# Instance norm over 512 channels: loads of two units at once on SP's queue, and the last unit's sum divided between VectorE and ScalarE

## The chip, the cores and the metric

One core of a Trainium2 chip. The metric is the device time of one execution in microseconds (us); lower is better. The median of 3 runs of the kernel before is 626.86 us (626.76 to 626.9).

## What is computed

x has the shape 4 x 8 x 16 x 256 x 256 in float32: 512 channels of 65,536 values, 134 MB. Each channel is shifted by its mean, divided by its standard deviation and multiplied by a gamma of its own (128 gammas, one for each group and channel):

```python
mu = x.mean(axis=(3, 4), keepdims=True)
var = ((x - mu) ** 2).mean(axis=(3, 4), keepdims=True)
out = (x - mu) / np.sqrt(var + 1e-5) * gamma[None, :, :, None, None]
```

The result is as large as x, so 268 MB have to pass between HBM and the core's own memory, half in and half out.

## The kernel before

The work is cut into 32 units. A unit is 16 channels: each channel is spread over 8 partitions (S = 8), so that a unit fills a tile of 128 partitions x 8192 float32, 4 MB, a row of 32 KB in each partition. In HBM a unit is one contiguous block, and unit u + 1 lies 4 MB behind unit u. The core's memory holds six such tiles, the slots (AHEAD = 6); unit u uses slot u mod 6 from its load to the end of its store.

For each unit, in the loop over u:

- VectorE sums each partition's row (L107), and beside it ScalarE squares the row and sums the squares with its accumulator (L108). ScalarE's output proper goes to a tile, junk, that nobody reads.
- TensorE multiplies the two columns of sums with a matrix that adds the 8 partitions of each channel and divides by the number of values, with a minus sign (L116). The result is in PSUM.
- VectorE makes the negative variance (L117), ScalarE its root (L121), VectorE the reciprocal (L125) and the product with gamma (L127).
- VectorE normalises the tile in place (L130).
- ScalarE's queue issues the store (L134), and SP's queue issues the load of unit u + 6 into the same slot (L48).

The order on each engine is the order of the program text. That matters in two places. ScalarE issues the store of unit u, for which it waits until VectorE has normalised the unit, before it squares unit u + 1. And VectorE normalises unit u before it sums unit u + 1. SP has nothing but loads; the load of unit u + 6 waits until the store of unit u has landed.

At the start all six slots are loaded at once: units 1 and 3 are issued on ScalarE's queue, the other four on SP's (L48, called from the loop in L56 and L57). Ahead of them GpSimd's queue gets two small transfers, a write of 16 x 512 bytes of zeros into the output of unit 0 (L54, from the tile touch that VectorE clears in L53; the store of unit 0 later covers it) and the load of gamma (L55). Then the constants are made while the first units are on their way.

All transfers run on the same 16 DMA engines. The profile calls SP's queue q1, ScalarE's q10 and GpSimd's q0.

Of the kernel before, what the change touches and what calls it, by code (L numbers as in the profile page):

```python
# [1 line left out]

# [4 lines left out]

F32 = mybir.dt.float32
U8 = mybir.dt.uint8
ALU = mybir.AluOpType  # L10
ACTF = mybir.ActivationFunctionType
AX = mybir.AxisListType


@with_exitstack
def kernel(
    ctx: ExitStack,
    tc: tile.TileContext,
    x: bass.AP,
    gamma: bass.AP,  # L20
    out: bass.AP,
):
    nc = tc.nc
    B, G, C, H, W = x.shape
    P = nc.NUM_PARTITIONS
    HW = H * W
    n_ch = B * G * C
    S = 8
    K = P // S
    F = HW // S  # L30
    U = n_ch // K
    NG = (G * C) // K
    AHEAD = 6
    assert HW % S == 0 and (G * C) % K == 0

    xv = x.rearrange("b g c h w -> (b g c h w)").rearrange("(u p f) -> u p f", p=P, f=F)
    ov = out.rearrange("b g c h w -> (b g c h w)").rearrange("(u p f) -> u p f", p=P, f=F)
    gv = gamma.rearrange("g c -> (g c)")

    data = ctx.enter_context(tc.tile_pool(name="data", bufs=1))  # L40
    singles = ctx.enter_context(tc.tile_pool(name="singles", bufs=1))
    psum = ctx.enter_context(tc.tile_pool(name="psum", bufs=4, space=bass.MemoryType.PSUM))
    ctx.enter_context(tc.manual_schedule())

    slots = [data.tile([P, F], F32, name=f"xt{i}") for i in range(AHEAD)]

    def load(u, queue):
        queue.dma_start(out=slots[u % AHEAD][:], in_=xv[u])  # L48


    g_row = singles.tile([1, G * C], F32, name="g_row")
    touch = singles.tile([16, 128], F32, name="touch")
    nc.vector.memset(touch[:], 0.0)  # L53
    nc.gpsimd.dma_start(out=ov[0][0::S, 0:128], in_=touch[:])  # L54
    nc.gpsimd.dma_start(out=g_row[:], in_=gv[None, :])  # L55
    for u in range(AHEAD):  # L56
        load(u, nc.scalar if u in (1, 3) else nc.sync)  # L57

    for _ in range(60):
        nc.scalar.nop()  # L60

    eps_t = singles.tile([P, 1], F32, name="eps_t")
    nc.gpsimd.memset(eps_t[:], 1e-5)
    one = singles.tile([1, 1], F32, name="one")
    nc.gpsimd.memset(one[:], 1.0)
    navg = singles.tile([P, K, S], F32, name="navg")
    nc.gpsimd.memset(navg[:], -1.0 / HW)  # L67
    nc.gpsimd.affine_select(  # L68
        out=navg[:], in_=navg[:], pattern=[[-S, K], [0, S]], compare_op=ALU.is_ge,
        fill=0.0, base=0, channel_multiplier=1,  # L70
    )
    nc.gpsimd.affine_select(  # L72
        out=navg[:], in_=navg[:], pattern=[[S, K], [0, S]], compare_op=ALU.is_ge,
        fill=0.0, base=S - 1, channel_multiplier=-1,
    )
    navg_w = navg[:].rearrange("p k s -> p (k s)")
    root_eps = singles.tile([P, 1], F32, name="root_eps")
    nc.scalar.activation(out=root_eps[:], in_=eps_t[:], func=ACTF.Sqrt)  # L78
    g_rep = singles.tile([1, NG, K, S], F32, name="g_rep")
    g_ps = psum.tile([P, NG], F32, name="g_ps", bufs=1)  # L80
    g_col = singles.tile([P, NG], F32, name="g_col")

    nc.vector.tensor_copy(  # L83
        out=g_rep[:],
        in_=g_row[:].rearrange("o (n k) -> o n k", n=NG).unsqueeze(3).to_broadcast([1, NG, K, S]),
    )
    for n in range(NG):
        nc.tensor.matmul(  # L88
            out=g_ps[:, n : n + 1],
            lhsT=g_rep[:, n].rearrange("o k s -> o (k s)"),  # L90
            rhs=one[:],
            start=True, stop=True,
        )
    nc.vector.tensor_copy(out=g_col[:], in_=g_ps[:])  # L94

    junk = singles.tile([P, F], U8, name="junk")

    st = singles.tile([P, U, 2], F32, name="st")
    nvar = singles.tile([P, U], F32, name="nvar")
    std = singles.tile([P, U], F32, name="std")  # L100
    rstd = singles.tile([P, U], F32, name="rstd")
    scale = singles.tile([P, U], F32, name="scale")

    squares = []
    for u in range(U):
        t = slots[u % AHEAD]
        nc.vector.reduce_sum(out=st[:, u, 0:1], in_=t[:], axis=AX.X)  # L107
        square = nc.scalar.activation(  # L108
            out=junk[:], in_=t[:], func=ACTF.Square, accum_out=st[:, u, 1:2],
        )  # L110
        if u:

            tc.declare_no_dep(square.ins, squares[-1].ins, reason="junk, ordered by the root between")
        squares.append(square)
        ps = psum.tile([P, 2], F32, name="ps")
        nc.tensor.matmul(out=ps[:], lhsT=navg_w, rhs=st[:, u], start=True, stop=True)  # L116
        nc.vector.tensor_scalar(  # L117
            out=nvar[:, u : u + 1], in0=ps[:, 0:1], scalar1=ps[:, 0:1],
            scalar2=ps[:, 1:2], op0=ALU.mult, op1=ALU.add,
        )  # L120
        nc.scalar.activation(  # L121
            out=std[:, u : u + 1], in_=nvar[:, u : u + 1], func=ACTF.Sqrt,
            bias=eps_t[:], scale=-1.0,
        )
        nc.vector.reciprocal(out=rstd[:, u : u + 1], in_=std[:, u : u + 1])  # L125
        g = u % NG
        nc.vector.tensor_mul(  # L127
            out=scale[:, u : u + 1], in0=rstd[:, u : u + 1], in1=g_col[:, g : g + 1],
        )
        nc.vector.tensor_scalar(  # L130
            out=t[:], in0=t[:], scalar1=ps[:, 0:1], scalar2=scale[:, u : u + 1],
            op0=ALU.add, op1=ALU.mult,
        )
        nc.scalar.dma_start(out=ov[u], in_=t[:])  # L134
        if u + AHEAD < U:
            load(u + AHEAD, nc.sync)


# [1 line left out]
_INS = ['x', 'gamma']  # L140
_OUTS = [((4, 8, 16, 256, 256), 'float32')]


# [23 lines left out]
```

## Time and profile before

The profiled execution is known by its span, from the first to the last instruction; no other time of it is given. The span is 624.9 us; the median of the runs is 1.95 us above it.

| | us or share |
|---|---|
| median of 3 runs | 626.86 |
| span of the profiled execution | 624.9 |
| VectorE busy | 443.4 (71%) |
| ScalarE busy | 238.8 (38%) |
| TensorE busy | 21.4 (3%) |
| DMA, mean over the span | 430 GB/s |
| one sum of a unit, VectorE (L107) | 8.69 |
| one square of a unit, ScalarE (L108) | 7.03 |
| one normalisation of a unit, VectorE (L130) | 4.55 |
| VectorE idle, waiting for loads (L107) | 100.4 |
| ScalarE idle, waiting for loads (L108) | 231.9 |

How to read it: a busy share is an average over stages with different limits. An engine that waits for a load is not what bounds the kernel at that moment. The slices of the page give, for each of 40 equal parts of the span, the busy share of each engine in tenths, and for the DMA engines also what they moved in GB/s. The timeline tells when an instruction started, how long it took and, in brackets, how long its engine had been idle and what ended that.

### The profile page before, as it was taken

To read this page: it belongs to the slowest core of one execution; us is meant where nothing else is said; L and a number is where in the kernel's file an instruction comes from. 1 tells how busy PE (TensorE), PEld (TensorE's weight loads), DVE (VectorE), ACT (ScalarE), POOL (GpSimd) and SP (SyncE) were. 2 spreads that over 40 slices of the span, in tenths; PEclk is the share of its full clock that TensorE was granted. 3 is DMA by queue.
4 is the path that set the end of the run, shared out by engine and by line. 5 is a ranking of instruction groups with operands and counts; after the bars stand their busy time and mean duration, and the time that the engine had idled before them with its cause. 6 is when DMAs were issued, how large, how long until landed. Compare 5 with 4: busy or idle time off the path is not lost.

```text
span 624.9 us, 631 instructions
## 1 busy us (share of the span) xinstructions
PE 21.4 (3%) x80; PEld 19.5 (3%) x80; DVE 443.4 (71%) x163; ACT 238.8 (38%) x98; POOL 2.4 (0%) x11
## 2 busy tenths in 40 slices
PE   0200000000000000000000000000000000000000
PEld 0200000000000000000000000000000000000000
DVE  0588999999776687666786767867668676687730
ACT  0444444444443234432344423444224442244400
POOL 1000000000000000000000000000000000000000
DMA  8999999999999999999999999999999999999998
GB/s 370 436 426 430 422 434 436 436 436 437 432 424 433 436 436 424 436 436 434 436 436 432 422 436 436 434 426 436 436 434 436 436 434 419 436 436 434 426 436 369
DMA packets 9282, 268.46 MB, mean 430 GB/s; under 512 B 1072, under 2 KB 1088, under 8 KB 1088
## 3 DMA queue, kind: packets, MB, share of 16 engines
q10 hardware_dynamic: 4896, 142.61, 52.9%
q1 hardware_dynamic: 4320, 125.83, 46.8%
q0 software_dynamic: 64, 0.01, 0.0%
q14 instruction: 2, 0.02, 0.0%
HBM read 134.22 MB, written 134.23 MB: 430 GB/s over the span
## 4 chain that ended last, share of the span: by engine, by line
another core or an unknown queue 61%; DMA 17%; DVE 15%; SPq 1%; PE 1%; issue 0%; ACT 0%
DVE st L107 10%; DMA xt<-in_x_dram 10%; DMA out_dram<-xt 8%; DVE xt L130 5%; SPq L48 1%; PE ps L116 1%; ACT std L121 0%; DVE nvar L117 0%; DVE rstd L125 0%; DVE scale L127 0%
## 5 line engine op out<-in xcount | busy, mean ns | idle before, releaser
L107 DVE TENSOR_REDUCE st<-xt 128x1 f32<-128x8192 f32 x32 | 277.9, 8685 | 100.4 <-DMA xt<-in_x_dram 100.4
L108 ACT ACTIVATE junk<-xt 128x8192 uint8<-128x8192 f32 x32 | 225.0, 7030 | 275.1 <-DMA xt<-in_x_dram 231.9
L130 DVE TENSOR_SCALAR xt<-xt,ps,scale 128x8192 f32<-128x8192 f32 x32 | 145.6, 4550 | 1.2
L121 ACT ACTIVATE std<-nvar,eps_t 128x1 f32<-128x1 f32 x32 | 9.4, 294 | 79.6 <-DVE nvar L117 79.6
L116 PE MATMUL ps<-st,navg 128*128 128x2 f32 x64 | 17.9, 349 | 557.1 <-DVE st L107 557.1
L116 PEld LDWEIGHTS ps<-st,navg 128*128 128x128 f32 x64 | 16.0, 311 | 558.9 <-issue 558.9
L117 DVE TENSOR_SCALAR nvar<-ps 128x1 f32<-128x1 f32 x32 | 9.2, 287 | 23.8 <-PE ps L116 23.8
L125 DVE RECIPROCAL rstd<-std 128x1 f32<-128x1 f32 x32 | 5.2, 164 | 11.6 <-ACT std L121 11.6
L83 DVE COPY g_rep<-g_row 1x1024 f32<-1x1024 f32 x1 | 0.7, 681 | 14.3 <-DMA g_row<-in_gamma_dram 14.3
L108 ACT ACTIVATION_READ_ACCUMULATOR junk<-xt 128x1 f32 x32 | 6.0, 186 | 0.0
L127 DVE TENSOR_TENSOR scale<-rstd,g_col 128x1 f32<-128x1 f32 x32 | 5.1, 159 | 1.1
L88 PE MATMUL g_ps<-one,g_rep 1*128 1x1 f32 x16 | 3.5, 347 | 16.1 <-DVE g_rep L83 16.1
L88 PEld LDWEIGHTS g_ps<-one,g_rep 1*128 1x128 f32 x16 | 3.5, 325 | 16.1 <-issue 16.1
L94 DVE COPY g_col<-g_ps 128x8 f32<-128x8 f32 x1 | 0.2, 166 | 3.7 <-PE g_ps L88 3.7
L78 ACT ACT_TABLE_LOAD x1 | 1.3, 1283 | 1.7 <-PEq L151 1.7
L53 DVE MEMSET touch<- 16x128 f32 x1 | 0.2, 165 | 0.9 <-PEq L151 0.9
L54 POOL DMA_DIRECT2D out_dram<-touch x1 | 0.6, 619 | 0.8 <-DVE touch L53 0.8
L55 POOL DMA_DIRECT2D g_row<-in_gamma_dram x1 | 0.5, 487 | 0.0
L68 POOL TENSOR_SCALAR_AFFINE_SELECT navg<-navg 128x128 f32<-128x128 f32 x1 | 0.4, 400 | 0.1
L72 POOL TENSOR_SCALAR_AFFINE_SELECT navg<-navg 128x128 f32<-128x128 f32 x1 | 0.4, 399 | 0.1
L67 POOL MEMSET navg<- 128x128 f32 x1 | 0.2, 232 | 0.0
L78 ACT ACTIVATE root_eps<-eps_t 128x1 f32<-128x1 f32 x1 | 0.2, 203 | 0.0
(6 smaller groups left out, 0.6 us busy)
## 6 DMA issues: line engine op xcount, KB each, us to landing
out_dram<-xt ACTq DMA_DIRECT2D x32, 4096.0 KB, 62.5
xt<-in_x_dram SPq DMA_DIRECT2D x30, 4096.0 KB, 38.5
xt<-in_x_dram ACTq DMA_DIRECT2D x2, 4096.0 KB, 31.5
out_dram<-touch POOLq DMA_DIRECT2D x1, 8.0 KB, 9.1
g_row<-in_gamma_dram POOLq DMA_DIRECT2D x1, 0.5 KB, 13.3
```

What stands on the lines that cost most here:

```text
L48: queue.dma_start(out=slots[u % AHEAD][:], in_=xv[u])
L78: nc.scalar.activation(out=root_eps[:], in_=eps_t[:], func=ACTF.Sqrt)
L83: nc.vector.tensor_copy(out=g_rep[:], in_=g_row[:].rearrange("o (n k) -> o n k", n=NG).unsqueeze(3).to_broadcast([1, NG, K, S]),)
L88: nc.tensor.matmul(out=g_ps[:, n : n + 1], lhsT=g_rep[:, n].rearrange("o k s -> o (k s)"), rhs=one[:], start=True, stop=True,)
L107: nc.vector.reduce_sum(out=st[:, u, 0:1], in_=t[:], axis=AX.X)
L108: square = nc.scalar.activation(out=junk[:], in_=t[:], func=ACTF.Square, accum_out=st[:, u, 1:2],)
L116: nc.tensor.matmul(out=ps[:], lhsT=navg_w, rhs=st[:, u], start=True, stop=True)
L117: nc.vector.tensor_scalar(out=nvar[:, u : u + 1], in0=ps[:, 0:1], scalar1=ps[:, 0:1], scalar2=ps[:, 1:2], op0=ALU.mult, op1=ALU.add,)
L121: nc.scalar.activation(out=std[:, u : u + 1], in_=nvar[:, u : u + 1], func=ACTF.Sqrt, bias=eps_t[:], scale=-1.0,)
L125: nc.vector.reciprocal(out=rstd[:, u : u + 1], in_=std[:, u : u + 1])
L127: nc.vector.tensor_mul(out=scale[:, u : u + 1], in0=rstd[:, u : u + 1], in1=g_col[:, g : g + 1],)
L130: nc.vector.tensor_scalar(out=t[:], in0=t[:], scalar1=ps[:, 0:1], scalar2=scale[:, u : u + 1], op0=ALU.add, op1=ALU.mult,)
```

## The change

All loads take two units at once. Three tiles of 128 x 2 x 8192 take the place of the six slots, and a load fills both halves of one of them: 8 MB, in each partition two rows of 32 KB that lie 4 MB apart in HBM. All loads are issued by SP, the first three too. The load of units u + 6 and u + 7 (u even) is issued once, after the stores of units u and u + 1, so that it waits for both. The stores stay single, 4 MB each, on ScalarE's queue.

The write of zeros into the output, the tile touch and 60 empty instructions of ScalarE at the start go.

In the last unit (u = 31) VectorE sums the first half of each row only, 4096 values. ScalarE squares the whole row as before, and then copies the second half into junk with its accumulator on, which sums it. VectorE adds the two half sums. The rest is as it was.

```diff
-    slots = [data.tile([P, F], F32, name=f"xt{i}") for i in range(AHEAD)]
+    pairs = [data.tile([P, 2, F], F32, name=f"xt{i}") for i in range(AHEAD // 2)]
 
-    def load(u, queue):
-        queue.dma_start(out=slots[u % AHEAD][:], in_=xv[u])
+    def load(u):
+        nc.sync.dma_start(
+            out=pairs[(u % AHEAD) // 2][:], in_=xv[u : u + 2].rearrange("t p f -> p t f"),
+        )
...
-    touch = singles.tile([16, 128], F32, name="touch")
-    nc.vector.memset(touch[:], 0.0)
-    nc.gpsimd.dma_start(out=ov[0][0::S, 0:128], in_=touch[:])
     nc.gpsimd.dma_start(out=g_row[:], in_=gv[None, :])
-    for u in range(AHEAD):
-        load(u, nc.scalar if u in (1, 3) else nc.sync)
-
-    for _ in range(60):
-        nc.scalar.nop()
+    for u in range(0, AHEAD, 2):
+        load(u)
...
+    halves = singles.tile([P, 2], F32, name="halves")
...
-        t = slots[u % AHEAD]
-        nc.vector.reduce_sum(out=st[:, u, 0:1], in_=t[:], axis=AX.X)
+        t = pairs[(u % AHEAD) // 2][:, u % 2]
+        last = u == U - 1
+        if last:
+            nc.vector.reduce_sum(out=halves[:, 0:1], in_=t[:, : F // 2], axis=AX.X)
+        else:
+            nc.vector.reduce_sum(out=st[:, u, 0:1], in_=t, axis=AX.X)
         square = nc.scalar.activation(
-            out=junk[:], in_=t[:], func=ACTF.Square, accum_out=st[:, u, 1:2],
+            out=junk[:], in_=t, func=ACTF.Square, accum_out=st[:, u, 1:2],
         )
...
+        if last:
+            nc.scalar.activation(
+                out=junk[:, F // 2 :], in_=t[:, F // 2 :], func=ACTF.Copy, accum_out=halves[:, 1:2],
+            )
+            nc.vector.tensor_add(out=st[:, u, 0:1], in0=halves[:, 0:1], in1=halves[:, 1:2])
...
-        nc.scalar.dma_start(out=ov[u], in_=t[:])
-        if u + AHEAD < U:
-            load(u + AHEAD, nc.sync)
+        nc.scalar.dma_start(out=ov[u], in_=t)
+        if u % 2 and u - 1 + AHEAD < U:
+            load(u - 1 + AHEAD)
```

## The prediction

> **What bounds the kernel now.** First the page's slices, queues and issues: do the 16 DMA engines ever rest?
>
> ```profile
> DMA  8999999999999999999999999999999999999998
> GB/s 370 436 426 430 422 434 436 436 436 437 432 424 433 436 436 424 436 436 434 436 436 432 422 436 436 434 426 436 436 434 436 436 434 419 436 436 434 426 436 369
> ...
> q10 hardware_dynamic: 4896, 142.61, 52.9%
> q1 hardware_dynamic: 4320, 125.83, 46.8%
> ...
> out_dram<-xt ACTq DMA_DIRECT2D x32, 4096.0 KB, 62.5
> xt<-in_x_dram SPq DMA_DIRECT2D x30, 4096.0 KB, 38.5
> ```
>
> They don't. q1 is SP's queue, q10 ACT's (32 stores and two loads). A 4 MB transfer at 434 GB/s needs 9.7 us alone, 19.3 us with the other queue beside it; loads land after 38.5 us and stores after 62.5 us, so both queues hold work waiting. Stretch by stretch (us from the span's start; then busy us of each engine, clock, DMA share, GB/s) the last 38 us, when only stores are left, are as full as the middle:
>
> ```profile
> 44.00:157.00 113.00, 4.47 (x16) 4.02 (x16) 103.57 (x40) 53.41 (x24) 0.00 (x0) 1.00 1.01 434
> 157.00:584.00 427.00, 12.27 (x44) 11.02 (x44) 304.75 (x111) 163.16 (x66) 0.00 (x0) 1.00 1.00 433
> 584.00:622.00 38.00, 0.56 (x2) 0.50 (x2) 13.85 (x5) 7.42 (x3) 0.00 (x0) 1.00 1.01 435
> ```
>
> The DMA packet records give the account. Every packet of data is one row of 32 KB; on one engine rows follow each other every 1.209 us. 64 transfers x 8 rows per engine x 1.209 = 618.8 us. The first rows start at 2.06 us on average (issued at 0.80) and take 1.69 us instead of 1.21, 0.5 more. When the first store starts (39.8 to 43 us) rows are slow once more, 0.64 us per engine. A completion write costs (19.365 us per unit - 16 x 1.2086)/2 = 0.013 us, 0.8 for 64. Sum 622.8; the records end at 623.07 on average, 623.60 at the latest; the span ends 1.3 later, at 624.9. The median of the runs, 626.86, is 1.95 above this span; I add 1.95 to every span.
>
> Now the tail, in the timeline (start, duration, instruction). The last load releases VectorE and ScalarE at 585.26, and its store is issued at 600.32:
>
> ```profile
> 585.26 7.03 ACT L108 ACTIVATE junk<-xt 128x8192 uint8<-128x8192 f32 x1 [9.33 <-DMA xt<-in_x_dram]
> 585.26 8.69 DVE L107 TENSOR_REDUCE st<-xt 128x1 f32<-128x8192 f32 x1 [4.35 <-DMA xt<-in_x_dram]
> ...
> 595.73 4.55 DVE L130 TENSOR_SCALAR xt<-xt,ps,scale 128x8192 f32<-128x8192 f32 x1
> 600.32 0.34 ACTq L134 DMA_DIRECT2D out_dram<-xt  x1
> ```
>
> At 584 exactly 28 stores (0 to 27) are done and three (28, 29, 30) are queued behind them: 29 us of store work, to 613, so the last unit's 15 us of arithmetic are hidden with 13 us to spare.
>
> **The change, part by part.** *What the transfers cost.* Bytes and row size stay, so the 618.8 us stay. 16 transfers fewer take 16 x 0.013 = 0.2 us off. The first pair has SP's queue to itself, 16 rows at full rate, where units 0 and 1 shared the engines row by row: compute starts at 22.6 us either way. The slow rows at the first store (0.64 us) may stay or go, as no row shows a first store without the warm-up write; I take -0.3, bounds 0 and -0.64. The warm-up write itself, the memset and the nops go at no gain: they lie beside the first load.
>
> *Order in the middle.* The rows of the two queues alternate one by one: on q10 rows start at 43.00 and 45.42, on q1 at 44.21 between them. So 16 rows of a pair's load run beside two stores of 8. A pair's load waits on SP for the later of two stores; before, each slot was freed by its own store. The store queue then still holds two stores, 19 us, against SP's reaction (landing 158.9, issue 159.6, first row about 1 us on): under 2 us in which q1 is empty and q10 works. Hidden, unless q10 ran empty too. SP carries nothing but loads, so nothing else waits behind it. Since load and store pairs have equal rows, and a late load is waited for, they settle in step: when the last pair lands, 28 stores are done, as before (bounds 224 to 225 rows per engine: 0 to +1.2 us). The last load thus releases compute at 585.3 - 0.2 - 0.3 = 584.8.
>
> *The tail.* But now **two** units land then, not one, with only stores 28 and 29 (16 rows, 19.3 us) to cover them. Unit 30 takes the 15.02 us shown above: normalised at 599.8, issued in time (16 rows end at 603). Store 30 runs to 613. Unit 31 comes behind 30, and its order is that of the early stretch, where two units lie ready:
>
> ```profile
> 37.56 8.68 DVE L107 TENSOR_REDUCE st<-xt 128x1 f32<-128x8192 f32 x1
> 37.68 0.35 ACTq L134 DMA_DIRECT2D out_dram<-xt  x1
> 38.08 7.03 ACT L108 ACTIVATE junk<-xt 128x8192 uint8<-128x8192 f32 x1 [5.41 <-DVE xt L130]
> 45.01 0.19 ACT L108 ACTIVATION_READ_ACCUMULATOR junk<-xt 128x1 f32 x1
> ```
>
> ScalarE issues store 30 before it squares unit 31, so the square starts 0.43 us after unit 30 is normalised (37.65 to 38.08) and ends with its accumulator at +7.55. Behind it on the same engine stands the new copy of half a unit, ordered after the square by the junk tile: no row shows it; half of the square's 7.03 is 3.5 (bounds 3.4 and 4.0, with accumulator and wait +0.3): +11.4. VectorE's half sum is over by +4.4 and waits. Then the addition (0.16, as the scale row) and hand-over, and from the sum to normalised 1.78 + 4.55 (593.95 to 600.28 above): +17.9. Undivided, the sum would have started at once and the unit ended at +14.9: **the division costs 3.0 us**, as ScalarE already has the square to do. Store 31 is issued at 599.8 + 17.95 = 617.75. Its first rows start 1.26 later, as the first load's did (bounds 1.0 and 1.9), 619.0; 8 rows, 9.67; a slow first row, 0 to 0.5, I take 0.2: 628.9, where before has 623.07. The engines rest from 613 to 619. That is **+5.8 us**, less 0.2 as a fresh start leaves less scatter between engines than 623.60 - 623.07. Span 624.9 + 5.6 = 630.5, time **632.5**.
>
> **Rivals.** *Loads get more than every second row* (0.09). If one turn of a queue held both rows of a partition, or a whole transfer's share, 16 load rows would pass beside 8 store rows, the last pair would land 8 x 1.209 = 9.7 us earlier, the chain would end by 619.2, and the full queues would end last: 623.07 - 0.5, time about 626.3: no change. It decides from 16 load rows to 10.9 store rows on. The one-row turns above speak against it, but there a partition had one row per transfer. The Trainium skill, page "DMA: Bandwidth & Descriptors", section "Queues, rings and completion order", has an engine drain a whole packet, typically 9 to 17 descriptors, before it changes queue. By that rule a pair's load gives 17 and a store 9 per turn, and the time is this rival's; the records at 43 to 45 us contradict it for transfers of 9.
>
> *The new loads are slow* (0.03). Two neighbouring rows of a load now lie 4 MB apart. Were its 256 rows per engine as slow as the first ones (1.69), it would cost 256 x 0.48 = 123 us, about 750. The Trainium skill, same page, section "Latency and other measured facts", measured half the rate for rows 4 MiB apart. Against it: up to 38 us units 0 and 1, then 2 and 3, were read in just such alternation, and the 36 us from 2 to 38 moved 429 GB/s.
>
> *SP's wait shows* (0.05). If q10 were empty in its 2 us too, 13 pairs would pay up to 26 us: up to 658. Two queued stores speak against it.
>
> *The division does what it says* (0.05). If the square of 31 overlapped unit 30's arithmetic, the 3.0 us would go, or with 4.4 for the half sum all that the engines rest: 626.3 to 629.5. The order on ScalarE speaks against it.
>
> **How the numbers follow.** The forecast has 0.78. Its bounds: landing -0.35 to +1.7, copy -0.4 to +0.5, first row -0.5 to +0.8: about 630.8 to 635.3; taken down to 630.0 for part of the last rival. The rest, below 0.2, is left out. A measurement of this kernel can tell about 0.2%, 1.25 us, from no change. Slower by more: the forecast, slow loads, SP's wait and half of the last rival, 0.88; within: most of the first rival and a little of the last, 0.09; faster 0.03.
>
> **What would show it.** In the profile after: DMA full until about 613, then some 6 us of nothing, one store last, and a chain that ends in the half copy, the last unit's normalisation and its store; the last pair lands near 585; the copy near 3.6 us with VectorE waiting for it; middle stretches at 433 or 434 GB/s. Wrong it would be if the last pair lands near 575 (turns), if the middle falls below 430 (slow loads, SP's wait), or if the copy runs before store 30 is issued.

## The result

The changed kernel takes 634.79 us (median of 4 runs, 634.44 to 635.28), beside 626.88 us of the kernel before: ratio 1.0124, 95% interval 1.0111 to 1.0136. It is 7.9 us slower; 5.6 us were forecast, in a range that holds the time.

The page of the changed kernel, with the span, the slices and the three rows of the last unit's divided sum; last, the issues with the median us to landing:

```profile
span 633.6 us, 618 instructions
...
DMA  8999999999999999999999999999999999999986
GB/s 372 434 389 443 441 432 422 432 434 430 434 408 432 431 439 434 431 432 437 430 432 437 430 430 432 439 437 430 432 437 430 432 434 432 430 432 437 434 345 265
...
L120 DVE TENSOR_TENSOR st<-halves 128x1 f32<-128x1 f32 x1 | 0.2, 160 | 7.0 <-ACT junk L117 7.0
L106 DVE TENSOR_REDUCE halves<-xt 128x1 f32<-128x4096 f32 x1 | 4.4, 4410 | 0.0
...
L117 ACT ACTIVATE junk<-xt 128x4096 uint8<-128x4096 f32 x1 | 3.6, 3617 | 0.0
...
xt<-in_x_dram SPq DMA_DIRECT2D x16, 8192.0 KB, 41.6
out_dram<-xt ACTq DMA_DIRECT2D x32, 4096.0 KB, 39.2
```

Up to the last two slices the DMA row is the one of before; there it falls to 8 and 6, at 345 and 265 GB/s. VectorE stands idle for 7.0 us ahead of the addition (L120): it waits for ScalarE's half copy. By stretches (DMA share and GB/s are the last two numbers):

```profile
180.00:584.00 404.00, 11.72 (x42) 10.53 (x42) 287.37 (x105) 153.75 (x63) 0.00 (x0) 1.00 1.00 433
584.00:614.00 30.00, 0.56 (x2) 0.50 (x2) 18.17 (x6) 17.55 (x6) 0.00 (x0) 1.00 1.01 435
616.00:622.00 6.00, 0.00 (x0) 0.00 (x0) 4.87 (x3) 0.25 (x1) 0.00 (x0) 1.00 0.00 1
```

The middle is as full as before. From 616 to 622 the engines move nothing, while VectorE finishes unit 31. The timeline tells what they wait for:

```profile
588.40 8.69 DVE L108 TENSOR_REDUCE st<-xt 128x1 f32<-128x8192 f32 x1 [8.76 <-DMA xt<-in_x_dram]
...
598.87 4.55 DVE L136 TENSOR_SCALAR xt<-xt,ps,scale 128x8192 f32<-128x8192 f32 x1
603.34 4.41 DVE L106 TENSOR_REDUCE halves<-xt 128x1 f32<-128x4096 f32 x1
603.45 0.34 ACTq L140 DMA_DIRECT2D out_dram<-xt  x1
603.84 7.03 ACT L109 ACTIVATE junk<-xt 128x8192 uint8<-128x8192 f32 x1 [5.39 <-DVE xt L136]
...
610.99 3.62 ACT L117 ACTIVATE junk<-xt 128x4096 uint8<-128x4096 f32 x1
...
614.73 0.16 DVE L120 TENSOR_TENSOR st<-halves 128x1 f32<-128x1 f32 x1 [6.99 <-ACT junk L117]
...
616.93 4.55 DVE L136 TENSOR_SCALAR xt<-xt,ps,scale 128x8192 f32<-128x8192 f32 x1 [0.29 <-DVE scale L133]
621.52 0.34 ACTq L140 DMA_DIRECT2D out_dram<-xt  x1
```

The last pair releases VectorE at 588.40. Unit 30 is normalised by 603.42 and its store issued. Only then does ScalarE square unit 31 (603.84), and only then copy its half (610.99); VectorE's half sum was over at 607.75. Store 31 is issued 33.1 us after the landing, at 621.52; before it was 15.1 us, 600.32 after 585.26.

### The profile page after: what moved, and what is told of

It is laid out like the page before. It is cut to its first block, busy times and chain, and to the rows that moved or that the text cites. A ratio compares the mean times of both kernels' runs of the same rounds, so it can differ in the third digit from the quotient of the medians.

```text
span 633.6 us, 618 instructions
## 1 busy us (share of the span) xinstructions
PE 21.4 (3%) x80; PEld 19.5 (3%) x80; DVE 438.2 (69%) x163; ACT 242.5 (38%) x100; POOL 1.9 (0%) x10
## 4 chain that ended last, share of the span: by engine, by line
DMA 64%; DVE 29%; ACT 2%; PE 1%; issue 1%; ACTq 0%; SPq 0%
DMA xt<-in_x_dram 36%; DMA out_dram<-xt 28%; DVE st L108 18%; DVE xt L136 10%; PE ps L122 1%; ACT junk L109 1%; ACT std L127 1%; DVE nvar L123 1%; ACT junk L117 1%; DVE rstd L131 0%; DVE scale L133 0%; ACTq L140 0%; DVE st L120 0%; SPq L49 0%
## 5 line engine op out<-in xcount | busy, mean ns | idle before, releaser
L108 DVE TENSOR_REDUCE st<-xt 128x1 f32<-128x8192 f32 x31 | 269.1, 8682 | 126.2 <-DMA xt<-in_x_dram 126.2
L122 PEld LDWEIGHTS ps<-st,navg 128*128 128x128 f32 x64 | 16.0, 311 | 587.1 <-issue 587.1
L120 DVE TENSOR_TENSOR st<-halves 128x1 f32<-128x1 f32 x1 | 0.2, 160 | 7.0 <-ACT junk L117 7.0
L106 DVE TENSOR_REDUCE halves<-xt 128x1 f32<-128x4096 f32 x1 | 4.4, 4410 | 0.0
L117 ACT ACTIVATE junk<-xt 128x4096 uint8<-128x4096 f32 x1 | 3.6, 3617 | 0.0
```

Source lines behind the costliest of these rows:

```text
L106: nc.vector.reduce_sum(out=halves[:, 0:1], in_=t[:, : F // 2], axis=AX.X)
L108: nc.vector.reduce_sum(out=st[:, u, 0:1], in_=t, axis=AX.X)
L117: nc.scalar.activation(out=junk[:, F // 2 :], in_=t[:, F // 2 :], func=ACTF.Copy, accum_out=halves[:, 1:2],)
```

## The experiments

Theory A is the prediction's: the bytes move as before, but two units land at once at the end with two stores to cover them, and the division makes the second one later still, because ScalarE has the square to do behind store 30. Each time below stands beside 626.92 or 627.23 us of the kernel before on the same chip.

### The last unit summed whole

```diff
-        last = u == U - 1
+        last = False
```

> The changed kernel, but the last unit is summed whole by VectorE, as all others are. Theory A (two units land at once, the engines run dry, and the division costs time because ScalarE already has the square to do): VectorE sums unit 31 from 14.9 us after the last landing instead of waiting for ScalarE; store 31 is issued about 30.0 us after the landing instead of 33.1; time 634.8 - 3.1 = 631.7. Rival B (the division does what it says and the loss lies in the transfers): 634.8 + up to 4 us = 635 to 639. Rival C (the end is set by the transfers, not by the chain of work): 634.8, unchanged.

Measured: 632.5 us, ratio 1.009 (1.0073 to 1.0107). That is 2.3 us less than with the division. Its timeline:

```profile
587.62 8.69 DVE L108 TENSOR_REDUCE st<-xt 128x1 f32<-128x8192 f32 x1 [8.74 <-DMA xt<-in_x_dram]
...
602.56 8.68 DVE L108 TENSOR_REDUCE st<-xt 128x1 f32<-128x8192 f32 x1
...
617.61 0.34 ACTq L140 DMA_DIRECT2D out_dram<-xt  x1
```

VectorE sums unit 31 without a break after unit 30, and store 31 is issued 29.99 us after the landing instead of 33.12: the chain is 3.1 us shorter, as expected, and the medians differ by 2.3. Part of the rest is the last store itself: by the packet records the latest engine ends its last row 0.8 us after the mean of the 16 here (629.16 and 628.32), 0.1 us after it in the changed kernel (632.25 and 632.17). Rivals B and C fall. The other 5.6 us are still there, so the division is the smaller part of the loss.

### The last pair in two transfers

```diff
     def load(u):
+        if u == U - 2:
+            for i in range(2):
+                nc.sync.dma_start(out=pairs[(u % AHEAD) // 2][:, i], in_=xv[u + i])
+            return
```

> The changed kernel, but units 30 and 31 are loaded by two transfers of 4 MB, each behind its own store; all other loads stay 8 MB. Theory A: unit 30 lands some 19 us before unit 31, near 569, its arithmetic is hidden again, and store 31 is queued before the stores ahead of it are through (near 606, against 615); the DMA engines never rest and the last row ends about 1.4 us after that of the kernel before (the rows slow beyond those of before): 627.0 to 628.6. Rival (the 8 MB transfers themselves cost, over the whole run): most of the 7.9 us stays, 632 to 635.

Measured: 628.15 us, 1.0017 (1.0008 to 1.0026). One transfer cut in two takes 6.6 of the 7.9 us away, with the division still in place. From its timeline:

```profile
578.82 8.68 DVE L112 TENSOR_REDUCE st<-xt 128x1 f32<-128x8192 f32 x1
...
611.69 0.34 ACTq L144 DMA_DIRECT2D out_dram<-xt  x1
```

Unit 30 has landed at 568 (by the records' last completion write, the few bytes with which each engine ends its part of a transfer) and is summed at 578.82, as soon as VectorE is through with unit 29. Store 31 is issued at 611.69, before the stores ahead of it are out, and its stretches show no rest:

```profile
612.00:616.00 4.00, 0.00 (x0) 0.00 (x0) 0.00 (x0) 0.00 (x0) 0.00 (x0) 1.00 1.06 453
```

The rival, a cost of the 8 MB transfers over the whole run, keeps at most the 1.2 us that remain.

### The start alone

```diff
-    touch = singles.tile([16, 128], F32, name="touch")
-    nc.vector.memset(touch[:], 0.0)
-    nc.gpsimd.dma_start(out=ov[0][0::S, 0:128], in_=touch[:])
...
-        load(u, nc.scalar if u in (1, 3) else nc.sync)
-
-    for _ in range(60):
-        nc.scalar.nop()
+        load(u, nc.sync)
```

> The kernel before with the start of the changed one alone: all six first loads (4 MB each) on SP's queue, without the warm-up write and the empty instructions. Theory A: no tail, store 31 hidden; the slow rows around the first store grow from 0.7 to about 1.4 us per engine as in the changed kernel: 627.2 to 627.8. Rival (the start costs nothing and the slow rows of the changed kernel come from the 8 MB loads): 626.9, within 0.3.

This is the kernel before with that edit. Measured: 627.5 us, 1.0012 (1.0003 to 1.0021), so at most 1.3 us. From its timeline:

```profile
28.15 0.38 ACTq L128 DMA_DIRECT2D out_dram<-xt  x1
...
596.63 8.69 DVE L101 TENSOR_REDUCE st<-xt 128x1 f32<-128x8192 f32 x1 [4.35 <-DMA xt<-in_x_dram]
...
611.69 0.34 ACTq L128 DMA_DIRECT2D out_dram<-xt  x1
```

The first store is issued at 28.15 us, as unit 0 lands alone, and the slow rows lie at 29 to 33 us: they move with the first store. From 2 to 38 us the engines lose 1.9 us against 433.8 GB/s (16 rows of 32 KB every 1.2086 us), where the kernel before loses 0.7 there and 0.7 at 38 to 44 us. (Time lost is the length of a stretch less its bytes at that rate, by the packet records; here and below.) So the rival falls: these are loads of 4 MB, and from 2 to 44 us they lose as much as the loads of 8 MB do, 2.2 us in the changed kernel and 1.8 to 1.9 in its variants.

The last load also lands 11.4 us later than before (596.63 instead of 585.26): the stores began 9.5 us earlier, and when the rows of the last load end, 231.9 store rows per engine are done, where the kernel before has done 223.1. It costs nothing that can be told, as store 31 is issued at 611.69 and store 30 runs to 613.4 at least.

### Store 30 issued by SP

```diff
-        nc.scalar.dma_start(out=ov[u], in_=t)
+        (nc.sync if u == U - 2 else nc.scalar).dma_start(out=ov[u], in_=t)
```

> The changed kernel, but the store of unit 30 is issued by SP, which has nothing left to do then; on ScalarE the square of unit 31 and its half copy no longer stand behind that store. Theory A: ScalarE squares unit 31 from 10.1 us after the last landing, its half copy ends at about 21.0, VectorE's half sum at 19.4; store 31 is issued about 27.7 us after the landing instead of 33.1: 634.8 - 5.4 = 629.4, with the engines at rest for about 1 us. Rival (the order on ScalarE is not what makes the division late): 634.8, unchanged.

Measured: 629.11 us, 1.0036 (1.0023 to 1.0049): 5.7 us less than the changed kernel. Its timeline:

```profile
587.59 8.69 DVE L108 TENSOR_REDUCE st<-xt 128x1 f32<-128x8192 f32 x1 [8.76 <-DMA xt<-in_x_dram]
...
597.55 7.01 ACT L109 ACTIVATE junk<-xt 128x8192 uint8<-128x8192 f32 x1
...
602.64 0.36 SPq L140 DMA_DIRECT2D out_dram<-xt  x1
604.69 3.62 ACT L117 ACTIVATE junk<-xt 128x4096 uint8<-128x4096 f32 x1
608.43 0.16 DVE L120 TENSOR_TENSOR st<-halves 128x1 f32<-128x1 f32 x1 [1.48 <-ACT junk L117]
...
615.20 0.34 ACTq L140 DMA_DIRECT2D out_dram<-xt  x1
```

ScalarE squares unit 31 at 597.55, while VectorE is still about to normalise unit 30; VectorE's wait ahead of the addition falls from 6.99 to 1.48 us, and store 31 is issued 27.6 us after the landing. So it is the place of the store on ScalarE that made the division late.

### Store 30 issued by SP, the sum whole

Both edits above together.

> The changed kernel with the store of unit 30 issued by SP, and the last unit summed whole by VectorE. Theory A: ScalarE squares unit 31 early, but VectorE sums it from 14.9 to 23.6 us after the last landing either way, so that store 31 is issued 30.0 us after the landing, as with the whole sum alone: 632.5. The store's place then pays only together with the division (629.1). Rival (the early square itself, or the store on SP's queue, gives the gain): 629 to 630.

Measured: 632.33 us, 1.0074 (1.0048 to 1.01). The timeline:

```profile
587.64 8.69 DVE L108 TENSOR_REDUCE st<-xt 128x1 f32<-128x8192 f32 x1 [8.78 <-DMA xt<-in_x_dram]
...
597.59 7.01 ACT L109 ACTIVATE junk<-xt 128x8192 uint8<-128x8192 f32 x1
...
602.58 8.68 DVE L108 TENSOR_REDUCE st<-xt 128x1 f32<-128x8192 f32 x1
...
617.63 0.34 ACTq L140 DMA_DIRECT2D out_dram<-xt  x1
```

The square is early here too (597.59) and gains nothing: VectorE's whole sum ends last, and the store is issued 29.99 us after the landing, to the hundredth as with the whole sum alone. The four kernels make a table of medians:

| last unit | store 30 on ScalarE | store 30 on SP |
|---|---|---|
| divided | 634.79 | 629.11 |
| whole | 632.5 | 632.33 |

The division costs 2.3 us behind the store and gains 3.2 us ahead of it. By the timelines, from the last landing to the issue of store 31, it is 3.1 us of cost and 2.4 us of gain; the kernel before took 626.88 to 627.23 us beside the four, so a few tenths of these differences tell nothing.

### The warm-up write put back, and left out of the kernel before

```diff
+    touch = singles.tile([16, 128], F32, name="touch")
+    nc.vector.memset(touch[:], 0.0)
+    nc.gpsimd.dma_start(out=ov[0][0::S, 0:128], in_=touch[:])
     nc.gpsimd.dma_start(out=g_row[:], in_=gv[None, :])
```

> The changed kernel with the warm-up write of 16 x 512 bytes into the output put back (from GpSimd's queue, as before). Theory A (without it the rows around the first store are slower: 1.1 to 1.4 us of the engines' time lost at 38 to 44 us, against 0.7 before): the loss there goes back to about 0.7, the last pair lands 0.5 us earlier, 634.8 - 0.5 = 634.3. Rival (the write warms nothing; the loss comes from loads on one queue): loss 1.1 or more, 634.8.

> The kernel before without the warm-up write, nothing else. Theory A: the loss at 38 to 44 us grows from 0.7 to about 1.1 or more, 626.9 + 0.5 = 627.4. Rival (the two queues at the start keep it at 0.7, not the write): 626.9 within 0.2.

Measured: 634.44 us with the write put back into the changed kernel, 0.35 us less than without it, where the runs of either kernel lie 0.5 to 0.8 us apart. The engines lose 1.12 us at 38 to 44 us, within the 1.11 to 1.36 of the variants without the write (1.08 in the next variant, which has it too). And 627.24 us without it in the kernel before, 0.9996 (0.9984 to 1.0008), with 0.85 us lost there instead of 0.67. Theory A falls in this point: the write is worth nothing that these runs can tell. The larger loss goes with the start of all loads on one queue, and not with the write, nor with 8 MB: from 2 to 44 us it is 1.9 us with 4 MB loads that all start on SP's queue, and 1.3 and 1.5 where two of them start on ScalarE's, with the write and without it. (The 60 empty instructions, gone in the former, were not tried alone.)

### What is left of the change without its tail

The changed kernel with the last pair in two transfers, the sum whole and the warm-up write put back; the 8 MB loads up to unit 29 stay.

> The changed kernel with three parts undone: the last pair in two transfers of 4 MB, the last unit summed whole, the warm-up write put back. What stays is 8 MB loads up to unit 29, all on SP's queue. Theory A: no tail and the slow rows of the kernel before: 628.15 - 0.5 = 627.6; at best that of before, 626.9, as the same bytes go through engines that never rest. Rival (the 8 MB loads save completion writes and SP's work on top): below 626.5.

Measured: 628.23 us, 1.0009 (0.9997 to 1.0021). This can't be told from the kernel before, and an interval from 0.9997 on leaves the rival, below 626.5, no room. The mean of the last rows' ends is 623.74, against 623.07 before, but the latest engine ends at 625.24, against 623.60: the 16 engines are less in step. In the middle of the run the completion writes of one store lie up to 4.7 us apart from engine to engine here (in an execution that was the longest of the ten), 2.3 in the changed kernel, 2.1 with 4 MB loads that all start on SP's queue, and 0.9 in the kernel before.

No variant beat the kernel before, and the runs point to none that would: its engines already move bytes from 2 to 623 us.

## Why the prediction was right

**The bound.** As forecast, the middle kept 433 GB/s and the loss came at the end, as a stretch in which the engines rest.

**Transfers.** Nothing was gained: the 0.2 us of 16 fewer completion writes can't be seen. The slow rows at the first store did not shrink by the 0.3 us that I took; they grew by 0.4 to 0.7 us (0.67 to between 1.11 and 1.36 us lost at 38 to 44).

**Order in the middle.** Rows alternate one by one, now with 16-row loads too, and a pair takes 38.7 us (completion writes of its loads from 509.6, 548.3 and 587.1 on). SP's wait for two stores was hidden in the time, and shows in the order: where one pair's load ends and the next begins, no load row starts on any engine for 3.0 to 3.9 us (after 237.1 us, and so on to 546.9), and store rows go in their place. Part of the gap goes with the wait for the second store: it is 2.4 to 2.6 us at 546 us in the two variants in which the load of unit 30 waits for its own store alone. The kernels with 4 MB loads have none above 1.6 us. In step was not quite right: each load ends 3 to 4 us after the second store beside it, from 160 us on.

**The tail.** The half copy took 3.62 us against my 3.5, the chain from landing to store 33.12 against 32.97. The whole sum and SP's store show the 3.0 us of the division (3.1 in the timeline, 2.3 in the medians) and its reason, the order on ScalarE.

**Rivals.** Turns of more than a row did not come: the last pair landed at 588, not 575. By the rule of the Trainium skill, page "DMA: Bandwidth & Descriptors", section "Queues, rings and completion order", a turn would be a packet of 9 to 17 descriptors; the trace disagrees for loads of 8 MB as it did for 4 MB. Rows 4 MB apart cost nothing of size: 433 GB/s. The same page's section "Latency and other measured facts" has half the rate for tiles whose every row lies 4 MiB from the next; with only two rows so, no run here shows it.

**The term that was off.** It is the landing of the last pair: 584.8 forecast, 588.40 measured, beyond my bound of 586.5. At the mean end of the last load rows the engines had done 480.2 rows each, at 586.31 us; before, 479.0 at 583.12. The 3.2 us between are 1.2 store rows more (1.4 us; I had taken none, with one row as the bound), 0.7 more at the first store, 0.3 at 90 to 110 us, and 0.8 at 170 to 180 us. The last two belong to this one execution: the three kernels that differ only behind unit 29 (whole sum, store 30 on SP, both) lost at most 0.1 and 0.01 in these stretches, and released VectorE at 587.6, still beyond my bound.

The step that was off is "28 stores are done, as before". The 28 came out: 28 stores are 224 rows per engine, and 224.3 store rows are done at the mean end of the last load rows (224.7 to 225.1 in the variants with 8 MB loads). But in the kernel before it is 223.1 there; I read off the 28 at 584, 0.9 us behind that end, and so gave the extra row no time. Added up from 632.5: landing +3.6, chain +0.15, the first row of store 31 0.90 after its issue and not 1.26, -0.36, the last store -0.1, scatter at the end -0.25, and 1.7 outside the span instead of my 1.95, -0.25: 635.3, the time of the profiled execution (635.28).

That the range holds the time is in part luck. The landing went 1.9 us beyond its bound, and no other term came near its upper bound. The bounds as listed add up to 631.25 to 635.5, not to 630.8 to 635.3.

What stays open: why 1.2 store rows more go by, and 1.6 to 2.0 in the variants with 8 MB loads. A lead that is set at the start and then kept shows in one run, the start alone (8.8 rows), but with an earlier first store and 4 MB loads; the gap at the end of each pair's load could also do it. Neither was tried with 8 MB loads. Nor is it known why the engines fall out of step; the start of the run with 4 MB loads on SP's queue is enough for it.

## What to carry to other kernels

Where the DMA engines are the bound, look at what they still have queued when the last load lands: everything computed after that must be done before that queue runs dry, and a last load twice as large doubles the work while the cover shrinks. Make transfers small at the end, whatever their size in the middle. Work shared with a second engine is only sooner done if that engine is free then; read its program order, the stores it issues included, before counting on it.

## What was not expected of the hardware

In the changed kernel the first store is issued at 37.76 us, and its first row starts at 42.71; the last store's first rows start 0.90 us after its issue, on average. In those 5 us the load rows of the other queue slow down as well, up to 2.68 us a row instead of 1.21. Slow rows near the first store show in every kernel here; they moved with the first store, and a small earlier write to the same output changed nothing that could be measured.
